# A GEGLU MLP in fp16: the first pass fed by plain fp32 loads, weight operands stored in the second pass, x scaled by 1/16

## The chip, the cores and the metric

The kernel runs on one core of a Trainium2 chip. Times are device microseconds (us) of that core, medians of several runs in its normal ("fast") state; the runs of one kernel in one round lie within about 0.2% of each other. A profile is one execution, taken by the hardware profiler; its span is 1.8 us shorter than the time of the same run. Experiments marked "one look" have a single time, so that their state can't be told. Engines: TensorE (PE in the profile, PEld its weight loads), VectorE (DVE), ScalarE (ACT), GpSimd (POOL), and the DMA issuing queue of SyncE (SP). L12 is line 12 of the kernel shown.

## The reference

```python
# x: 8 x 1024 x 1024, w_gate and w_up: 1024 x 4096, w_down: 4096 x 1024, all fp32
gate = x @ w_gate
up = x @ w_up
gate = 0.5 * gate * (1 + np.tanh(np.sqrt(2 / np.pi) * (gate + 0.044715 * gate ** 3)))
h = gate * up
return (h @ w_down).astype(np.float32)
```

## The kernel before

The kernel takes the 8192 rows of x in eight passes of 1024. A pass has a gate/up stage of 16 pairs of weight blocks and a down stage. Every matrix product is done as a 2x2 block scheme with seven products instead of eight, so the matmuls need sums and differences of blocks: of x (`t1` to `t4`, once per pass), of the weights (`sums_w`), and of w_down (`wd_sums`). All matmuls are fp16, 128 rows by 512 columns.

Weights arrive as fp32 in memory. Before the change they are cast on the way by GpSimd DMAs; the finished operands (raw blocks and sums) are written to memory once and read back in later passes. x is cast in memory and then transposed by DMA.

```python
WSRC = 3
...
def cast_x(p):                       # fp32 -> fp16, in memory, 2 MiB
    nc.gpsimd.dma_start(out=xh[r, :], in_=x2[r, :])
def transpose_x(p):                  # four transposing DMAs
    for n, kh, mh in (...):
        nc.sync.dma_start_transpose(out=xq[n], in_=xh[...])
...
def load_w(p, i):
    for w in range(2):
        c = ring.tile([P, 4096], FP16, tag="ring", name="wc")      # 6 buffers: three pairs
        if from_source(p, i):
            nc.gpsimd.dma_start(out=raw(c), in_=w_v[w][:, :, ...])  # casting
        else:
            nc.sync.dma_start(out=c, in_=wop[w][i])
def from_source(p, i): return p < 2 or (p == 2 and i < NP // 2)
def keeps(p, i):       return (p == 1 and i >= NP // 2) or (p == 2 and i < NP // 2)
...
# in pass 0, eight times, once per 21 products: w_down is loaded (casting, GpSimd), summed on
# VectorE 14 to 17 products later, and stored from SP as seven transfers
(0, wd_load), (14, wd_sums 0), (15, wd_sums 1), (16, wd_sums 2), (17, wd_sums 3), (17, wd_store)
...
# in a pair: 14 products, each of 4 matmuls into a PSUM bank; a bank is accumulated over several
# products, and between two of them ScalarE copies it out ("snap")
after = {1: [snap s1 gate], 2: [snap s1 up], 4: [snap s2 gate], 5: [snap s2 up], 7: ..., 8: ...}
...
cast_x(0); load_w(0, 0); load_w(0, 1); transpose_x(0); sums_x(); sums_w(0, 0, 0); sums_w(0, 0, 1)
```

The order in the code is the order on each engine: nothing is rescheduled, and an engine's instruction that waits holds back all behind it.

## Time and profile before

| | before |
|---|---|
| time, median of 3 | 2420.92 us |
| span of the profile | 2422.5 us |
| TensorE busy | 2335.6 us (96%), 10752 matmuls |
| VectorE, ScalarE, GpSimd busy | 42%, 34%, 24% |
| operand stores | pass 1 (half), pass 2 (half) |

A busy share near 100% hides the losses. It is read better as a floor: what a stage takes beyond 0.2158 us for each of its matmuls is its loss. The **loss at the start** is the time at which the first product with a difference of x begins, less 8 x 0.2158 us for the eight matmuls that can run before it. The **loss of pass 0** is the time from there to the first matmul of the down stage, less 888 x 0.2158 = 191.6 us. Before, these times are 54.78 and 277.96 us: losses 53.1 and 31.5. Pass 1 loses nothing, pass 2 13.6, the end 4. All these losses come from one profile each, so differences of some 3 us between two profiles are not read.

### The profile page before, as it was taken

The page shows a single profiled execution, that of the slowest core. Times are in us where ns is not written, and L with a number is a line of the kernel's source. Part 1 is how long each engine was busy: PE and PEld are TensorE (multiplying, and loading weights), DVE is VectorE, ACT ScalarE, POOL GpSimd, SP SyncE. Part 2 cuts the span into 40 slices and gives each one's busy share as a digit, 9 for nine tenths or more (in the row PEclk, how much of TensorE's full clock was granted, in tenths as well). Part 3 has the DMA queues.
Part 4 walks back from the last instruction along what each step waited for, and adds up shares of the span by engine and source line. Part 5 has one row for each costly group of instructions (what it writes and reads, how often), then busy time and mean ns, then how long its engine had stood idle before and what let it go on. Part 6 is the DMA issues. An engine that isn't in the chain of part 4 may idle for free.

```text
span 2422.5 us, 27727 instructions
## 1 busy us (share of the span) xinstructions
PE 2335.6 (96%) x10752; PEld 1055.0 (44%) x10752; DVE 1027.3 (42%) x1504; ACT 830.1 (34%) x1410; POOL 577.8 (24%) x484
## 2 busy tenths in 40 slices
PE   1979999999998999999999999999999999999999
PEld 0434444444443444444444444444444444444444
DVE  1757625666163351333513344233522335233350
ACT  0434304442143421444114440244403443044420
POOL 1444203441042310333003330133201332023310
PEclk8989999999998999999999999999999999999999
DMA  9999666998797465544756455564645645554453
GB/s 152 180 204 211 177 195 97 175 262 272 170 272 239 174 218 194 204 185 174 225 194 206 177 186 193 215 209 176 206 166 221 210 175 187 210 197 174 175 187 109
DMA packets 230405, 469.49 MB, mean 194 GB/s; under 512 B 76160, under 2 KB 164224, under 8 KB 188800
## 3 DMA queue, kind: packets, MB, share of 16 engines
q1 hardware_dynamic: 142208, 400.59, 46.2%
q0 software_dynamic: 88064, 67.12, 19.1%
q8 instruction: 84, 1.38, 0.2%
q14 instruction: 49, 0.40, 0.1%
HBM read 436.21 MB, written 98.57 MB: 221 GB/s over the span
## 4 chain that ended last, share of the span: by engine, by line
PE 90%; DMA 7%; SPq 1%; DVE 1%; issue 0%; POOL 0%; ACT 0%; POOLq 0%; DVEq 0%; ACTq 0%
PE ps_a L241 33%; PE ps_da L375 18%; PE ps_b L241 17%; PE ps_db L375 9%; PE ps_c L241 8%; PE ps_dc L375 5%; DMA h_s<-in_w_down_dram 3%; DMA wd_ops<-h_s 2%; SPq L91 1%; DMA wc<-in_w_up_dram 1%; DMA x_half<-in_x_dram 1%; DMA x_b<-x_half 0%; SPq L189 0%; DVE t L255 0%; DVE h_s L170 0%
## 5 line engine op out<-in xcount | busy, mean ns | idle before, releaser
L241 PEld LDWEIGHTS <-wc 128*128 128x128 f16 x7168 | 704.3, 98 | 940.6 <-issue 63.3
L261 POOL TENSOR_TENSOR h_a<-t 128x512 f16<-128x512 f32 x384 | 496.7, 1294 | 1510.8 <-DVE t L255 1414.5
L241 PE MATMUL ps_a<-x_t,wc 128*128 128x512 f16 x3072 | 728.3, 380 | 12.4 <-ACT t L248 12.4
L248 ACT ACTIVATE t<-ps_a 128x512 f32<-128x512 f32 x768 | 458.0, 597 | 499.1 <-PE ps_a L241 499.1
L253 DVE TENSOR_TENSOR t<-ps_b,t 128x512 f32<-128x512 f32 x256 | 176.9, 691 | 691.6 <-ACT t L248 671.3
L375 PEld LDWEIGHTS <-h_a 128*128 128x128 f16 x3072 | 300.6, 98 | 362.5
L258 ACT ACTIVATE t<-t 128x512 f32<-128x512 f32 x384 | 240.9, 627 | 326.0 <-DVE t L253 325.3
L375 PE MATMUL ps_da<-dc,h_a 128*128 128x512 f16 x1536 | 335.4, 379 | 0.0
L347 ACT ACTIVATE o<-ps_da 128x512 f32<-128x512 f32 x128 | 76.4, 597 | 698.0 <-PE ps_da L375 698.0
L241 PE MATMUL ps_b<-x_t,wc 128*128 128x512 f16 x1024 | 264.5, 381 | 21.5 <-DVE wc L142 21.5
L241 PE MATMUL ps_a<-x_b,wc 128*128 128x512 f16 x1024 | 246.8, 385 | 29.8 <-DMA x_b<-x_half 29.8
L241 PE MATMUL ps_b<-x_b,wc 128*128 128x512 f16 x1024 | 246.2, 384 | 19.7 <-DVE t L253 19.7
L241 PE MATMUL ps_c<-x_b,wc 128*128 128x512 f16 x1024 | 262.8, 379 | 0.0
L375 PE MATMUL ps_db<-dc,h_a 128*128 128x512 f16 x1024 | 223.6, 379 | 0.0
L255 DVE SCALAR_TENSOR_TENSOR t<-ps_b,t 128x512 f32<-128x512 f32 x256 | 177.0, 691 | 40.1 <-PE ps_b L241 21.8
L350 DVE SCALAR_TENSOR_TENSOR o<-ps_db,o 128x512 f32<-128x512 f32 x64 | 44.3, 692 | 328.2 <-ACT o L347 244.9
L264 DVE SCALAR_TENSOR_TENSOR h_a<-ps_a,t 128x512 f16<-128x512 f32 x128 | 88.5, 691 | 83.3 <-PE ps_a L241 80.0
L375 PE MATMUL ps_dc<-dc,h_a 128*128 128x512 f16 x512 | 111.8, 379 | 0.0
L375 PE MATMUL ps_da<-dc,h_s 128*128 128x512 f16 x512 | 111.8, 379 | 0.0
L354 DVE TENSOR_TENSOR h_a<-h_a,h_a 128x2048 f16<-128x2048 f16 x96 | 110.2, 1214 | 0.0
L269 ACT ACTIVATE t<-ps_a 128x512 f32<-128x512 f32 x128 | 76.3, 596 | 65.6 <-PE ps_a L241 65.6
L255 DVE SCALAR_TENSOR_TENSOR t<-ps_c,t 128x512 f32<-128x512 f32 x128 | 88.4, 691 | 11.9
(26 smaller groups left out, 516.7 us busy)
## 6 DMA issues: line engine op xcount, KB each, us to landing
wc<-w_ops SPq DMA_DIRECT2D x176, 1024.0 KB, 6.4
dc<-wd_ops SPq DMA_DIRECT2D x112, 1024.0 KB, 6.5
out_dram<-o SPq DMA_DIRECT2D x128, 256.0 KB, 2.4
w_ops<-wc SPq DMA_DIRECT2D x32, 1024.0 KB, 9.1
wc<-in_w_gate_dram POOLq DMA_DIRECT2D x40, 512.0 KB, 8.0
wc<-in_w_up_dram POOLq DMA_DIRECT2D x40, 512.0 KB, 13.1
x_half<-in_x_dram POOLq DMA_DIRECT2D x8, 2048.0 KB, 15.2
wd_ops<-h_s SPq DMA_DIRECT2D x56, 256.0 KB, 7.8
```

Source lines behind the costliest of these rows:

```text
L241: nc.tensor.matmul(ps, lhs(k), rhs[:, k, :], start=(first and k == 0), stop=(k == KH - 1), skip_group_check=True,)
L248: nc.scalar.activation(tl((n, w)), bank["a", w], COPY, scale=1.0 if w == 0 else HSC)
L253: nc.vector.tensor_tensor(o, bank[b, w], o, ADD)
L255: nc.vector.scalar_tensor_tensor(o, bank[b, w], HSC, o, MUL, ADD)
L258: nc.scalar.activation(t[n, 0], t[n, 0], GELU)
L261: nc.gpsimd.tensor_tensor(hq[h][:, i, :], t[n, 1], t[n, 0], MUL)
L264: nc.vector.scalar_tensor_tensor(hq["a12"][:, i, :], bank["a", 1], HSC, t["gl21"], MUL, MUL)
L269: nc.scalar.activation(tl("gl21"), bank["a", 0], GELU)
L347: nc.scalar.activation(tl((n, g)), bank["a", g], COPY, scale=OSC)
L350: nc.vector.scalar_tensor_tensor(t[n, g], bank[b, g], OSC, t[n, g], MUL, ADD)
L354: nc.vector.tensor_tensor(hq[o][:, s, :], hq[a][:, s, :], hq[b][:, s, :], op)
L375: nc.tensor.matmul(bank[b, g], lhs[:, j, g * P : (g + 1) * P], dc[:, n, :], start=(first and j == 0), stop=(j == NP - 1), skip_group_check ...
```

## The change

Intent: let the first pass start sooner and keep GpSimd's casting queue free. x of pass 0 is loaded plainly and transposed on TensorE; the weights of pass 0 are loaded plainly into two fp32 staging buffers and cast on ScalarE; all 16 pairs of operands are stored in pass 1 and none in pass 2; and x is scaled by 1/16 so that the up branch needs no scale of its own.

```diff
+    stage = ctx.enter_context(tc.tile_pool(name="stage", bufs=2))
+    def scale_x():                       # passes 1 to 7, in the down stage
+        for n in ("b11", "b12", "b21", "b22"):
+            nc.vector.tensor_scalar(xq[n], xq[n], XSC, None, MUL)
+    def x0_transpose(mh, g):             # one block of 128 rows, eight of them
+        if g % 2 == 0:
+            nc.vector.tensor_scalar(h, f, XSC, None, MUL)      # cast
+        else:
+            nc.scalar.activation(h, f, COPY, scale=XSC)        # cast
+        for k in range(2 * KH):
+            nc.tensor.transpose(ps[:, k], h[:, k * P : (k + 1) * P], identity)
+        nc.vector.tensor_copy(xq[...][:, :, c], ps[:, 0:KH])
+        nc.scalar.copy(xq[...][:, :, c], ps[:, KH : 2 * KH])
 ... load_w
+            if p == 0:
+                f = stage.tile([P, 2 * KH, 2 * P], FP32, tag="stage", name="wf")
+                nc.sync.dma_start(out=f, in_=w_v[w][:, :, ...])
+            elif from_source(p, i):
+    def cast_w(i, w, kh):                # four a pair: after products 4, 7, 10 and 13, for pair i + 2
+            nc.scalar.copy(raw(chunks[0, i, w])[:, k], staged[i, w][:, k])
     def from_source(p, i):
-        return p < 2 or (p == 2 and i < NP // 2)
+        return p < 2
     def keeps(p, i):
-        return (p == 1 and i >= NP // 2) or (p == 2 and i < NP // 2)
+        return p == 1
 ... (scales: snap, add and h21 lose HSC, the GELUs get scale=16)
-    cast_x(0)
-    load_w(0, 0)
-    load_w(0, 1)
-    transpose_x(0)
 ...
+    x0_load(0, 0); x0_load(0, 1); load_w(0, 0); x0_load(0, 2); x0_load(0, 3)
+    for g in range(G): x0_load(1, g)
+    load_w(0, 1)
+    for g in range(G): x0_transpose(0, g)
+    for n in (0, 2, 1, 3): cast_w(0, n // 2, n % 2)
```

(Some statements are joined on one line here. The transposes of the second half of x, `x0_rest`, come after the second product of the first pair.)

More of the change, by code (lines that the diff above doesn't have):

```diff
@@ L6 @@
 from concourse._compat import with_exitstack
+from concourse.masks import make_identity
 FP32 = mybir.dt.float32
@@ L14 @@
 COPY = mybir.ActivationFunctionType.Copy
-HSC = 1.0 / 16.0
+XSC = 1.0 / 16.0
+GSC = 16.0
 OSC = 16.0
@@ L50 @@
     G = MH // P
-    WSRC = 3
     w_v = [w.rearrange("(kc k) n -> k kc n", k=P) for w in (w_gate, w_up)]
@@ L79 @@
     }
+    identity = const.tile([P, P], FP16, name="identity")
     ctx.enter_context(tc.manual_schedule())
+    make_identity(nc, identity)
     def cast_x(p):
@@ L93, in transpose_x, with sum_x, x0_load @@
             )
-    def sums_x():
-        t = nc.vector.tensor_tensor
-        t(xq["t1"], xq["b12"], xq["b11"], SUB)
-        t(xq["t2"], xq["b22"], xq["t1"], SUB)
-        t(xq["t3"], xq["b22"], xq["b12"], SUB)
-        t(xq["t4"], xq["b21"], xq["t2"], SUB)
+    def scale_x():
+        for n in ("b11", "b12", "b21", "b22"):
+            nc.vector.tensor_scalar(xq[n], xq[n], XSC, None, MUL)
+    def sum_x(n):
+        o, a, b = {
+            1: ("t1", "b12", "b11"), 2: ("t2", "b22", "t1"),
+            3: ("t3", "b22", "b12"), 4: ("t4", "b21", "t2"),
+        }[n]
+        nc.vector.tensor_tensor(xq[o], xq[a], xq[b], SUB)
+    x0_f32 = {
+        mh: hq[n].rearrange("p a b -> p (a b)").bitcast(FP32).rearrange(
+            "p (t k) -> p t k", t=G
+        )
+        for mh, n in ((0, "a11"), (1, "a21"))
+    }
+    x0_f16 = hq["a12"].rearrange("p (t a) b -> p t (a b)", t=2 * G)
+    def x0_load(mh, g):
+        r0 = mh * MH + g * P
+        nc.sync.dma_start(out=x0_f32[mh][:, g], in_=x2[r0 : r0 + P, :])
+    def x0_transpose(mh, g):
+        f, h = x0_f32[mh][:, g], x0_f16[:, mh * G + g]
+        if g % 2 == 0:
+            nc.vector.tensor_scalar(h, f, XSC, None, MUL)
+        else:
+            nc.scalar.activation(h, f, COPY, scale=XSC)
+        ps = psum.tile([P, 2 * KH, P], FP16, tag="ps", name="ps_x")
+        for k in range(2 * KH):
+            nc.tensor.transpose(ps[:, k], h[:, k * P : (k + 1) * P], identity)
+        c = slice(g * P, (g + 1) * P)
+        nc.vector.tensor_copy(xq["b11" if mh == 0 else "b12"][:, :, c], ps[:, 0:KH])
+        nc.scalar.copy(xq["b21" if mh == 0 else "b22"][:, :, c], ps[:, KH : 2 * KH])
     chunks = {}
+    staged = {}
     def raw(c):
@@ L118, in load_w @@
             chunks[p, i, w] = c
-            if from_source(p, i):
+            if p == 0:
+                f = stage.tile([P, 2 * KH, 2 * P], FP32, tag="stage", name="wf")
+                staged[i, w] = f
+                nc.sync.dma_start(out=f, in_=w_v[w][:, :, i * 2 * P : (i + 1) * 2 * P])
+            elif from_source(p, i):
                 nc.gpsimd.dma_start(
@@ L124, in load_w @@
                 nc.sync.dma_start(out=c, in_=wop[w][i])
+    def cast_w(i, w, kh):
+        if i < NP:
+            k = slice(kh * KH, (kh + 1) * KH)
+            nc.scalar.copy(raw(chunks[0, i, w])[:, k], staged[i, w][:, k])
     def from_source(p, i):
-        return p < 2 or (p == 2 and i < NP // 2)
+        return p < 2
     def keeps(p, i):
-        return (p == 1 and i >= NP // 2) or (p == 2 and i < NP // 2)
+        return p == 1
     def sums_w(p, i, w):
@@ L247, in snap @@
         def snap(n, w):
-            nc.scalar.activation(tl((n, w)), bank["a", w], COPY, scale=1.0 if w == 0 else HSC)
+            nc.scalar.copy(tl((n, w)), bank["a", w])
         def add(n, b, w):
             o = t[n, w]
-            if w == 0:
-                nc.vector.tensor_tensor(o, bank[b, w], o, ADD)
-            else:
-                nc.vector.scalar_tensor_tensor(o, bank[b, w], HSC, o, MUL, ADD)
+            nc.vector.tensor_tensor(o, bank[b, w], o, ADD)
         def gelu(n):
-            nc.scalar.activation(t[n, 0], t[n, 0], GELU)
+            nc.scalar.activation(t[n, 0], t[n, 0], GELU, scale=GSC)
         def prod(n, h):
@@ L263, in h21 @@
         def h21():
-            nc.vector.scalar_tensor_tensor(
-                hq["a12"][:, i, :], bank["a", 1], HSC, t["gl21"], MUL, MUL
-            )
+            nc.vector.tensor_tensor(hq["a12"][:, i, :], bank["a", 1], t["gl21"], MUL)
         def gelu21():
-            nc.scalar.activation(tl("gl21"), bank["a", 0], GELU)
+            nc.scalar.activation(tl("gl21"), bank["a", 0], GELU, scale=GSC)
         after = {
@@ L304, in gate_up @@
                 extra[5].append(lambda i=i: sums_w(p, i + 1, 1))
+            if p == 0 and i == 0:
+                extra[2].append(x0_rest)
             if p == 0:
+                for n, k in enumerate((4, 7, 10, 13)):
+                    extra[k].append(lambda i=i, n=n: cast_w(i + 2, n // 2, n % 2))
                 for q in range(8):
@@ L411, in down @@
                         if name == "P5":
-                            sums_x()
+                            scale_x()
+                            for n in range(1, 5):
+                                sum_x(n)
                 k = 2 * v + nb + 4
@@ L421, in down, with x0_rest @@
             f()
-    cast_x(0)
+    def x0_rest():
+        for g in range(G):
+            x0_transpose(1, g)
+        sum_x(1)
+        sums_w(0, 0, 0)
+        sum_x(2)
+        sums_w(0, 0, 1)
+        sum_x(3)
+        sum_x(4)
+        for n in range(4):
+            cast_w(1, n // 2, n % 2)
+    x0_load(0, 0)
+    x0_load(0, 1)
     load_w(0, 0)
+    x0_load(0, 2)
+    x0_load(0, 3)
+    for g in range(G):
+        x0_load(1, g)
     load_w(0, 1)
-    transpose_x(0)
-    sums_x()
-    sums_w(0, 0, 0)
-    sums_w(0, 0, 1)
+    for g in range(G):
+        x0_transpose(0, g)
+    for n in (0, 2, 1, 3):
+        cast_w(0, n // 2, n % 2)
     for p in range(NPASS):
```

## The prediction

> **What bounds the kernel now.** I read the page first: 2422.5 us, TensorE busy 96%, and a low row of PE digits only at the start. Then the chain of waits in order of time, for the pace of an undisturbed matmul; then a table by stage, the list of what TensorE waited for, the timeline of the start, and the DMA queues of the stretch that is worst.
>
> The chain shows blocks of 64 matmuls in the down stage:
>
> ```profile
> 291.94 13.81 PE ps_dc L375 x64
> 305.75 13.81 PE ps_da L375 x64
> ```
>
> 13.81/64 is 0.2158 us per matmul. There are 10752 of them, so 2320.3 us is the floor of this program on TensorE, and 102 us of the span are lost. The stage table says where (columns: window, its length, PE busy with the count of matmuls, granted clock, DMA share, GB/s):
>
> ```profile
> 0.00:60.00 60.00, 8.79 (x26) 0.83 1.05 153
> 60.00:250.00 190.00, 168.34 (x742) 0.94 1.07 193
> 250.00:700.00 450.00, 450.00 (x2087) 1.00 0.83 200
> 700.00:850.00 150.00, 139.53 (x634) 0.95 0.72 220
> 850.00:2422.50 1572.50, 1568.90 (x7270) 1.00 0.53 191
> ```
>
> Length minus count times 0.2158 us gives the losses: 54 us in the first 60, 30 us from 60 to 250 (the first pass), nothing from 250 to 700, 13 us from 700 to 850 (the third pass), 4 us at the end. The reader is to see that the DMA share is over 1 in both bad early stretches and that the other passes run at the floor. So only some 97 us can be won at all, and 84 of them lie where the change works.
>
> What TensorE waited for, over the whole run:
>
> ```profile
> PE ps_a L241 <- DMA x_b<-x_half: 29.8, 1, 29.8
> PE ps_b L241 <- DVE wc L142: 21.5, 1, 21.5
> PE ps_b L241 <- DVE t L253: 19.7, 4, 10.5
> PE ps_a L241 <- ACT t L248: 12.4, 4, 10.8
> ```
>
> The first two are one cause. The timeline shows x cast in memory, then transposed by four transfers that hold the queue for 34 us; VectorE starts its differences of x only then, and the weight sums stand behind them:
>
> ```profile
> 14.76 33.98 SPq L91 DMA_TRANSPOSE x_b<-x_half  x4
> 49.08 1.23 DVE L97 TENSOR_TENSOR x_t<-x_b,x_b 128x2048 f16<-128x2048 f16 x1 [49.08 <-DMA x_b<-x_half]
> 54.78 1.89 PE L241 MATMUL ps_b<-x_t,wc 128*128 128x512 f16 x4 [21.45 <-DVE wc L142]
> ```
>
> Only eight matmuls (1.7 us of work) come before 54.78, so 53 us are gone there. In the first pass the DMA queues are full (60 to 250):
>
> ```profile
> q0 software_dynamic: 30103, 22.71, 82.9%
> q1 hardware_dynamic: 10320, 13.90, 23.3%
> ```
>
> 82.9% and 23.3% of 190 us are 157 and 44 us, together 202 us of all 16 engines. The casting transfers write 22.71/157 = 144 GB/s, the plain stores 13.90/44 = 314 GB/s. VectorE waits for the w_down load (31.5 us in this stretch), holds back the additions that stand behind it, and TensorE then lacks a bank.
>
> **What the Trainium skill says.** (1) "TensorE: Matmul & The Clock Gate", section "Wait — 56ns, not 53.3ns?": warm matmuls of 512 columns start 215.7 ns apart, cold ones 426.7 ns. The trace agrees: 215.8 ns warm, and the first eight stand about 0.43 us apart. (2) "DMA: Bandwidth & Descriptors", section "SWDGE vs HWDGE vs iDMA": a cast in a DMA must be issued by GpSimd, a plain transfer can go over SP's hardware queue, and each DMA engine takes turns between its queues. The trace bears out that the casting queue is the dear one (144 against 314 GB/s); turns between queues it does not show directly. (3) "ScalarE: Activation LUTs", section "What ACT_TABLE_LOAD costs": an ACTIVATE takes 186 ns + 0.833 ns per element, so 1.04 us for 1024. The trace has 597 to 627 ns at 512 where the formula gives 613. (4) "VectorE: DVE Perf Modes", section "The perf-mode tier table": fp16 tensor_scalar of 2048 elements 693 ns, tensor_tensor 1224 ns; the trace has 1.22 us for the second, none of the first.
>
> **The change part by part.**
>
> *Start.* Removed: the cast of x in memory and four transposing transfers for pass 0. Added: eight plain loads of x (4 MiB) and two of the first weights (2 MiB), 8 casts (VectorE and ScalarE by turns), 64 transposes on TensorE, 16 evacuations, 4 weight casts. The transfer work up to the last of x is 6.3 MB. At the 314 GB/s of the plain stores that is 20 us; at the 6.55 MB in 58.1% of 30 us = 376 GB/s that the 8 KB rows of the later weight loads reach (window 1260 to 1290), 17 us. The first w_down load is now issued at the very start beside it: 1.05 MB at 144 GB/s, 7 us. With some 2.5 us before the first byte and 2 us to land, the last x is there at about 30 us. Behind it stand one cast (1 us), eight transposes (at most 0.11 us each, a quarter of a cold matmul), an evacuation (0.6), a difference of x (1.2) and a weight sum (0.4): 5 us. So the product that now starts at 54.8 starts at about 35. The eight matmuls before it and most transposes fit in the wait. Loss at that point 35 - 1.7 = 33.3; then 1.4 for the cold clock (before, 54.4 us are lost up to 60 and 53.05 up to 54.78) and 1 for short waits on the interleaved differences and sums: **about 36 us instead of 54**.
>
> *Rest of pass 0.* 26 weight loads lie between 60 and 250. As casts they write 13.6 MB at 144 GB/s: 95 us. As plain fp32 loads they write 27.3 MB: 87 us at 314 GB/s, 73 us at 376. The 202 us of transfer work become 180 to 194. That stretch of 190 us fitted 202 us of work (queues overlap, 1.06), so the new work needs 170 to 183 us, while TensorE needs 742 x 0.2158 = 160. Transfers still bound it, by 10 to 23 us instead of 30: I take **16**. The w_down loads also no longer queue behind weight casts in the software queue, which favours the lower end. Against it: the cast of the next x (2 MiB, 15.2 us to land) still falls in the fifth pair, and ScalarE gets four casts of 1.04 us per pair. It now has some 6.1 us (six copies of 0.6, four GELUs) of each 12.1 us pair; 10.3 us is 85%, so it is not the bound by throughput. But it is in order: the first cast of a pair stands between two bank copies.
>
> *Passes 1 and 2.* Before, eight pairs of pass 1 and eight of pass 2 keep operands (1 MiB stores, w_ops<-wc x32); now all 16 of pass 1 do. The 32 stores stay 32; the 80 casting loads become 32 plain fp32 loads in pass 0, 32 casting loads in pass 1, and 16 more loads of finished operands in pass 2. The 13 us of pass 2 arise where the x cast (fifth pair) meets loads and stores; pass 1 had the x cast without stores and lost nothing. So the wait moves to pass 1. There it has eight more such pairs behind it, each some 7.3 us of casting loads (1 MiB at 144 GB/s) and 5.6 us of plain ones (2 MiB at 376) = 12.9 us against 12.1: slightly over, as in pass 1 now, where overlap hid it. I take **16 us** there and 0 in pass 2.
>
> *Scaling.* The 691 ns additions stay 691 ns (tensor_tensor and scalar_tensor_tensor of this shape both have it), the copies lose their scale for nothing, GELU takes it for nothing. x gets four scalings of 0.69 us per pass, in a down stage where VectorE has room: 0 us. Pass 2 saves 64 weight sums of 0.42 us on VectorE: off the path, 0 us.
>
> Sum: 2320.3 + 36 + 16 + 16 + 4 = 2392 us in a profile, which runs 1 to 2 us above the median: **2391 us**, 1.2% faster.
>
> **The rivals.** (a) *ScalarE blocks in order.* Each weight load waits until its one of two staging buffers has been cast, about ten products (9 us) before the cast that needs it. A 1 MiB plain load lands in 5.8 to 6.5 us (the w_ops and wd_ops rows), but w_down stores (1.8 MB, 6 us) stand before it in the same SP queue every 1.5 pairs, and the x cast takes 15 us. Then the cast waits for its data and the bank copies wait behind it, though the weights are not due for another pair. Speaks for it: loads that landed in 8 to 13 us under load. Against: the queues are less full. If most of the eight w_down rounds cost 3 to 5 us, pass 0 loses 40 and the time is about 2415. (b) *Transfers are hidden after all*: at the high rate pass 0 loses 5, the start ends at 30 and pass 1 repeats 13: 2320 + 31 + 5 + 13 + 4 = 2373, the 2% mark. (c) *The start is not transfer-bound*: ScalarE has two x casts, four evacuations and four weight casts (8.6 us) before the first product and again before the first bank copy, with the second pair's weight loads waiting on it; if these do not overlap with the loads the start loss is 45 and the time 2400. (d) *Storing in all of pass 1* makes it transfer-bound: 0.8 us over 16 pairs on top of the x cast, 26 us instead of 16: 2401.
>
> **Range and chances.** The start must shrink by 10 to 26 us, as no chain of cast and transpose in memory is left; pass 0 may lie between 5 and 40; pass 1 between 10 and 26. These add to 2374 to 2412. Over 2% faster needs all three at their best: 0.09. Slower by 2% would need 65 us of new waits in pass 0: 0.02.
>
> **What would show it.** The start step: the product of the first x difference begins near 35 us, released by VectorE, with the last x landing near 30. The pass-0 step: from there to 250 the matmul count gives a loss of 10 to 23, the DMA share stays near 1, the software queue falls under 40% of the stretch. Rival (a): bank copies on ScalarE wait behind a weight cast that waits for a DMA from w_gate or w_up. Pass step: a stall near the fifth pair of pass 1, none in pass 2. The prediction is wrong if the plain 1 KB-row loads run well below 314 GB/s, if ScalarE's in-order waits reach TensorE in every pair, or if pass 1 falls behind from pair to pair.

## The result, and the profile after

The changed kernel takes **2431.97 us** (2431.69 to 2432.17), against 2420.92: 0.45% slower. Ratios here are the mean time of one kernel's fast runs over that of the other's fast runs of the same rounds, so not quite the ratio of the medians: 1.0045, 95% interval 1.0022 to 1.0068. It is a small loss where 1.2% of gain was forecast, and it lies outside the stated range of 2374 to 2412.

The table by stage of the changed kernel (window, length, PE busy with count, clock, DMA share, GB/s). The first row's count holds 64 transposes:

```profile
0.00:60.00 60.00, 30.05 (x148) 0.89 0.73 228
60.00:250.00 190.00, 146.50 (x623) 0.90 0.95 249
250.00:700.00 450.00, 444.37 (x2052) 1.00 0.85 231
700.00:850.00 150.00, 150.00 (x697) 1.00 0.52 192
850.00:2429.90 1579.90, 1576.08 (x7303) 1.00 0.53 191
```

The first 60 us now lose 42 us instead of 54 (84 real matmuls), the next 190 lose 56 instead of 30, 250 to 700 loses 7 instead of nothing, and 700 to 850 loses nothing instead of 13. By stage, with the exact starts:

| loss, us | start | pass 0 | pass 1 | pass 2 | end | sum |
|---|---|---|---|---|---|---|
| before | 53.1 | 31.5 | 0 | 13.6 | 3.7 | 102 |
| predicted | 33.3 | 18.4 | 16 | 0 | 4 | 72 |
| after | 38.4 | 59.9 | 7.1 | 0 | 4.0 | 109 |

(In the prediction, 2.4 us of its "start" of 36 come after the first product of a difference; they are put to pass 0 here.) What TensorE waits for, after:

```profile
PE ps_a L286 <- ACT t L293: 43.5, 10, 14.3
PE ps_x L132 <- DVE h_a L127: 16.9, 3, 10.6
PE ps_x L132 <- ACT h_a L129: 8.4, 4, 2.1
PE ps_b L286 <- DVE t L297: 5.6, 1, 5.6
```

The waits for x and for VectorE have shrunk, and one for ScalarE's bank copies (L293) has grown from 12.4 to 43.5 us. What ScalarE itself waits for in the first 330 us names the next link:

```profile
ACT wc L169 <- DMA wf<-in_w_gate_dram: 46.3, 9, 14.7
...
ACT wc L169 <- DMA wf<-in_w_up_dram: 4.2, 4, 2.6
```

L169 is the cast of a staged weight. The longest case, in the timeline (start, duration, engine, what):

```profile
107.38 2.09 SPq L234 DMA_DIRECT2D wd_ops<-h_s  x3
...
109.51 1.05 ACT L169 CAST wc<-wf 128x1024 f16<-128x1024 f32 x1
...
110.58 0.38 SPq L158 DMA_DIRECT2D wf<-in_w_gate_dram  x1
...
120.00 1.03 PE L286 MATMUL ps_a<-x_t,wc 128*128 128x512 f16 x4
...
133.76 1.04 ACT L169 CAST wc<-wf 128x1024 f16<-128x1024 f32 x1 [14.65 <-DMA wf<-in_w_gate_dram]
134.71 1.06 ACT L293 COPY t<-ps_a 128x512 f32<-128x512 f32 x2
135.34 1.86 PE L286 MATMUL ps_a<-x_t,wc 128*128 128x512 f16 x4 [14.32 <-ACT t L293]
```

The buffer is free when the cast ends at 110.56, the load goes out at 110.58, and its data are there at 133.7, 23 us later. The cast waits for it, the copy of the bank waits behind the cast, and TensorE waits for the copy. The weights concerned are for the pair after next: no matmul needs them yet.

Is it that the transfers have no time left? The whole of pass 0, from the first product of a difference to the down stage, before and after (the same columns as above; both windows end a matmul late, hence 889):

```profile
54.78:278.12 223.34, 201.67 (x889) 0.94 0.99 188
```

```profile
40.09:291.74 251.65, 207.66 (x889) 0.91 0.85 232
```

Share times length is 221 us of all 16 engines before and 214 after: the work is a little less, but now it is spread over 28 us more, with 15% of the engines' time unused. That speaks against a plain lack of bandwidth and for loads that go out or land too late. The trace has both. From the third pair on, eight of the 28 weight loads went out 1.4 to 7.9 us after the end of the cast that freed their buffer, 36 us in all; the other 20 went out within 0.1 us. Of the 50.5 us that ScalarE waited for weights, 20.0 stand before casts whose load went out late, 30.5 before casts whose load went out at once and landed late. The experiments test it.

### The profile page after: what moved, and what is told of

It is laid out like the page before. It is cut to its first block, busy times and chain, and to the rows that moved or that the text cites. A ratio compares the mean times of both kernels' runs of the same rounds, so it can differ in the third digit from the quotient of the medians.

```text
span 2429.9 us, 27885 instructions
## 1 busy us (share of the span) xinstructions
PE 2347.0 (97%) x10816; PEld 1060.8 (44%) x10816; DVE 1023.4 (42%) x1480; ACT 887.5 (37%) x1486; POOL 536.9 (22%) x437
## 4 chain that ended last, share of the span: by engine, by line
PE 91%; DMA 6%; ACT 1%; DVE 1%; issue 1%; SPq 0%; POOL 0%; DVEq 0%; ACTq 0%; POOLq 0%
PE ps_a L286 34%; PE ps_da L419 18%; PE ps_b L286 17%; PE ps_db L419 9%; PE ps_c L286 9%; PE ps_dc L419 5%; DMA wf<-in_w_gate_dram 4%; DMA wc<-in_w_up_dram 1%; DMA h_a<-in_x_dram 1%; DMA wf<-in_w_up_dram 1%; ACT wc L169 0%; ACT t L293 0%; PE ps_x L132 0%; DVE t L297 0%; DVE h_s L215 0%
## 5 line engine op out<-in xcount | busy, mean ns | idle before, releaser
L286 PE MATMUL ps_a<-x_t,wc 128*128 128x512 f16 x3072 | 735.6, 382 | 44.0 <-ACT t L293 43.5
L297 DVE TENSOR_TENSOR t<-ps_b,t 128x512 f32<-128x512 f32 x512 | 353.1, 691 | 814.9 <-ACT t L293 772.0
L293 ACT COPY t<-ps_a 128x512 f32<-128x512 f32 x768 | 448.1, 585 | 428.6 <-PE ps_a L286 428.5
L286 PE MATMUL ps_c<-x_b,wc 128*128 128x512 f16 x1024 | 267.7, 385 | 0.0
L297 DVE TENSOR_TENSOR t<-ps_c,t 128x512 f32<-128x512 f32 x256 | 175.8, 687 | 14.0 <-PE ps_c L286 1.5
L306 DVE TENSOR_TENSOR h_a<-ps_a,t 128x512 f16<-128x512 f32 x128 | 88.5, 691 | 84.5 <-PE ps_a L286 82.9
L309 ACT ACTIVATE t<-ps_a 128x512 f32<-128x512 f32 x128 | 76.4, 597 | 71.3 <-PE ps_a L286 71.1
L169 ACT CAST wc<-wf 128x1024 f16<-128x1024 f32 x64 | 64.9, 1044 | 50.5 <-DMA wf<-in_w_gate_dram 46.3
```

Of the source, the lines that this page charges most:

```text
L169: nc.scalar.copy(raw(chunks[0, i, w])[:, k], staged[i, w][:, k])
L286: nc.tensor.matmul(ps, lhs(k), rhs[:, k, :], start=(first and k == 0), stop=(k == KH - 1), skip_group_check=True,)
L293: nc.scalar.copy(tl((n, w)), bank["a", w])
L297: nc.vector.tensor_tensor(o, bank[b, w], o, ADD)
L306: nc.vector.tensor_tensor(hq["a12"][:, i, :], bank["a", 1], t["gl21"], MUL)
L309: nc.scalar.activation(tl("gl21"), bank["a", 0], GELU, scale=GSC)
```

## The experiments

Theory W: pass 0 loses because ScalarE waits, in order, for plain weight loads that land late. Rival T: the transfers of pass 0 are too much, whoever issues them. Within W three causes were to be told apart: the small staging, the x cast of 2 MiB beside the loads, and the queue in which the loads stand. All results, with losses as defined above:

| kernel | time | start | pass 0 | pass 1 | pass 2 |
|---|---|---|---|---|---|
| before | 2420.92 | 53.1 | 31.5 | 0 | 13.6 |
| after | 2431.97 | 38.4 | 59.9 | 7.1 | 0 |
| e1 casting loads | 2395.87 | 30.9 | 30.5 | 9.0 | 0 |
| e2 half tiles | 2416.18 | 39.1 | 43.6 | 7.8 | 0 |
| e3 casts of x first (one look) | 2423.74 | 30.8 | 59.8 | 6.8 | 0 |
| e4 wait moved to GpSimd (one look, wrong result) | 2410.19 | 33.5 | 43.4 | 6.9 | 0 |
| e5 six half tiles (one look) | 2412.75 | 39.6 | 38.6 | 8.2 | 0 |
| e6 = e1 + e3 | 2391.98 | 24.8 | 33.9 | 7.2 | 0 |
| e7 before + stores in pass 1 | 2414.08 | 50.6 | 34.4 | 7.7 | 0 |
| e8 = e6 + late x cast | 2373.25 | 24.9 | 22.1 | 1.3 | 0 |
| e9 after + late x cast | 2416.52 | 38.9 | 53.1 | 0.9 | 0 |
| e10 = e2 + e3 + e9 | 2385.35 | 30.4 | 28.5 | 0.7 | 0 |
| e11 loads on ScalarE's queue (one look) | 2406.26 | 39.7 | 31.9 | 8.3 | 0 |
| e12 half the bytes (one look, wrong result) | 2398.70 | 36.3 | 28.6 | 7.5 | 0 |
| e13 = e11 + e3 + e9 | 2383.26 | 32.2 | 24.6 | 0.7 | 0 |

The kernel before, run beside them, took 2420.2 to 2421.9 us.

### e1: casting loads in pass 0

```diff
-            if p == 0:
-                f = stage.tile(...); nc.sync.dma_start(out=f, in_=w_v[w][...])
-            elif from_source(p, i):
+            if from_source(p, i):        # and cast_w does nothing
```

> The changed kernel with one part undone: the weights of pass 0 come again by casting GpSimd transfers, no staging, no casts on ScalarE; the new start, the stores in pass 1 alone and the scaling stay. Theory W (in pass 0 ScalarE waits in order for fp32 weight loads that land late): the loss of pass 0 goes back from 60 us to the 30 of the kernel before, so about 2400 us, faster than both. Rival T (the new start with its w_down loads and stores merely crowds the transfers that follow it): pass 0 still loses over 45 us, about 2420.

Measured: 2395.87 us, ratio to before 0.9899 (0.9884 to 0.9914). Pass 0 is back at 30.5. So the new start, the scaling and the stores in pass 1 are a gain of 24 us together (against the kernel before in the same round), and the plain weight loads alone cost 36 us (35 between the profiles: 29.4 in pass 0 and 7.5 at the start, less 1.9 in pass 1). T in the form "the new start crowds what follows" falls.

### e2, e5: finer and deeper staging

```diff
-                f = stage.tile([P, 2 * KH, 2 * P], FP32, ...)        # two of 1 MiB
+                for kh in range(2):
+                    f = stage.tile([P, KH, 2 * P], FP32, ...)        # e2: four, e5: six of 512 KB
+                    nc.sync.dma_start(out=f, in_=w_v[w][:, kh * KH : (kh + 1) * KH, ...])
```

(e5 takes its memory from the pool of bank copies, 14 to 11; passes 3 to 7 lose nothing by it.)

> The same staging memory cut into four half tiles, each loaded by a transfer of 512 KB as soon as its own half has been cast: the load of a half may be issued a whole pair (14 products) before its cast instead of 10 to 11. Same bytes. Theory W, window: ScalarE's wait for weight loads falls from 50 us to under 25 and the time to 2405 to 2418. Rival T (the transfer engines have no time left): within 5 us of the changed kernel.

> Half tiles with six buffers instead of four (8 KB a partition more, taken from the pool of bank copies, 14 to 11). The transfer work of pass 0 is the same 214 us of all engines. Theory W: with loads issued 1.5 pairs ahead the engines stay full, pass 0 takes about 214 to 225 us and loses 22 to 33 instead of 60 (43.6 with four half tiles): span 2395 to 2405. Rival T: no further gain over four half tiles, span 2412 to 2418. If the smaller copy pool hurts, passes 3 to 7 show it.

Measured: pass 0 loses 43.6 and 38.6. In e2 ScalarE still waits 40 us for weights (27.6 gate, 12.7 up), more than the 25 forecast, though the time is in the forecast window. e5 stops short of the 22 to 33 forecast: 50% more buffers bring only 5 us. The window of staging is a part of the cause, 16 to 21 us of it, and not the whole; in e5 ScalarE's longest wait, the one beside the x cast, is 14.5 us, as in the changed kernel (14.7).

### e4: the wait moved off ScalarE

The casts read a constant tile, so that they never wait; GpSimd copies one element of each staged tile instead, and paces the loads. To make room for the constant tile, the pool of bank copies goes from 14 to 13.

```diff
-            nc.scalar.copy(raw(chunks[0, i, w])[:, k], staged[i, w][:, k])
+            nc.scalar.copy(raw(chunks[0, i, w])[:, k], fixed)
+            if kh == 1:
+                nc.gpsimd.tensor_copy(seen[:, 0:1], staged[i, w][:, 0, 0:1])
```

> Wrong result on purpose: ScalarE casts a constant tile, so it never waits for a weight load; the loads stay, and GpSimd copies one element of each staged tile in ScalarE's place, so the loads are paced as before and the wait lies on GpSimd. If ScalarE's wait in front of the bank copies is what holds TensorE, TensorE's wait for bank copies (43.5 us) goes to under 10 us and the span to 2380 to 2400. If the transfers hold everything (through w_down and its sums on VectorE), the span stays over 2415.

Measured: neither. The span is 2408.4 and pass 0 loses 43.4. TensorE still waits 32.2 us for bank copies, but ScalarE no longer waits for weights; VectorE waits for w_down, first 330 us:

```profile
DVE h_s L220 <- DMA h_s<-in_w_down_dram: 34.4, 7, 14.2
```

So taking the weight wait off ScalarE is worth 16.5 us, and then the chain of w_down (load, sums, stores, next load) is the next bound by the waits that the trace shows; in the kernel before VectorE waits 31.5 us for w_down between 60 and 250. GpSimd, which now waits for the weights, also issues the w_down loads, so this run makes that chain somewhat later than it need be; it is not a clean measure of the floor.

### e11: the queue of the loads

Same buffers, same bytes, same casts; each load is issued from ScalarE, on ScalarE's own hardware queue, right behind the cast that frees its buffer. It no longer stands behind the w_down stores in SP's queue (the expectation calls that theory HOL, head of line): the trace lists these loads under a queue of their own, q10, beside SP's q1.

```diff
             nc.scalar.copy(raw(chunks[0, i, w])[:, k], staged[i, w][:, k])
+            if kh == 1 and i + 1 < NP:
+                load_f(i + 1, w, nc.scalar)      # was nc.sync, in load_w
```

> The plain weight loads of pass 0 issued on ScalarE's own hardware queue, right behind the cast that frees their buffer, so that they stand behind no w_down store in SP's queue. Theory HOL (the stores in front, and SP waiting for the sums to store, make the loads late): ScalarE's wait for weight loads falls from 50 to under 30 and pass 0 loses under 48. Rival: bandwidth and window alone; pass 0 loses 54 to 66 as before.

Measured: pass 0 loses 31.9 instead of 59.9, one look, 2406.26 us. ScalarE's wait for weight loads falls from 50.5 to 22.0 us:

```profile
ACT wc L176 <- DMA wf<-in_w_up_dram: 13.5, 5, 9.7
ACT wc L176 <- DMA wf<-in_w_gate_dram: 8.5, 4, 2.8
```

and TensorE's for bank copies from 43.5 to

```profile
PE ps_a L295 <- ACT t L302: 21.5, 9, 9.0
```

The pass, by its stage line, is also denser than in the changed kernel (share 0.92 instead of 0.85):

```profile
41.38:264.95 223.57, 200.60 (x888) 0.97 0.92 258
```

This is the largest effect of any single edit that leaves the bytes as they are, and nearly the whole of the 28.4 us by which pass 0 had become worse. The bytes stay, so the cause lies in when the loads go out and land. The queue is not the only way to mend that: the window (e2), the queue and the late x cast (e9) are worth 16.3, 28.0 and 6.8 us of pass 0 one by one, more together than the 28.4, so they overlap; and e10 below brings pass 0 to 28.5 on SP's queue. The changed kernel's SP queue shows both ways in which it acts:

```profile
55.16 6.56 SPq L234 DMA_DIRECT2D wd_ops<-h_s  x7
61.82 0.40 SPq L158 DMA_DIRECT2D wf<-in_w_gate_dram  x1
...
78.58 8.91 SPq L234 DMA_DIRECT2D wd_ops<-h_s  x7
87.59 0.39 SPq L158 DMA_DIRECT2D wf<-in_w_gate_dram  x1
```

The load at 61.82 goes out as soon as its buffer is free, but seven stores (1.8 MB) went out just before it on the same queue: it takes 14.9 us to land. The buffer of the load at 87.59 is free at 79.71, when its cast ends; but SP then stands in the seven stores, which wait for VectorE's sums, and issues the load 7.9 us late. The two were not tested apart, but the traces say which one e11 removes: every load now goes out within 0.03 us of the end of the cast before it, where 36 us of delay stood, while the mean time to landing of the loads from the third pair on hardly moves (10.3 us in the changed kernel, 9.7 in e11; the longest 24.5 and 21.6).

### e12: half the bytes

```diff
-                nc.sync.dma_start(out=f, in_=w_v[w][:, :, ...])
+                nc.sync.dma_start(out=f[:, 0:KH], in_=w_v[w][:, 0:KH, ...])   # both casts read this half
```

> Wrong result on purpose: each plain weight load of pass 0 brings only the first half of its rows and both casts read that half; every wait, queue and instruction stays, half of the 33 MB of weight reads goes. If the bytes of the loads make the loss, pass 0 falls from 60 to under 25. If the order of waits and the x cast make it, pass 0 still loses 35 or more.

Measured: 28.6, between the two. Half the bytes also land sooner (6.3 us in the mean instead of 10.3), so this run alone does not part W from T; with e11, which has all the bytes and loses 31.9, it does: the bytes fit, if they are not held up.

### e9, e8: the cast of the next x

The cast of the next pass's x in memory (2 MiB on GpSimd's queue) moves from the fifth pair to the fifteenth in passes 0 and 1, its transposes and sums accordingly later in the down stage.

```diff
-            if i == 4 and p + 1 < NPASS:
+            if i == (14 if p < 2 else 4) and p + 1 < NPASS:
                 extra[2].append(lambda: cast_x(p + 1))
...
-                        if name == "P1":          # transposes;  sums: "P5" -> "P3"
+                        if name == ("P6" if p < 2 else "P1"):
```

> The changed kernel with only the late cast of x (as in e8): plain weight loads, staging and ScalarE casts stay. In the changed kernel one weight load beside the x cast took 23 us to land and TensorE stood 14.3 us. Theory: the 2 MiB cast holds the engines against the plain loads; pass 0 loses 40 to 46 instead of 60 and pass 1 under 3, about 2405 to 2412. Rival (the loads are late anyway, the cast only happened to be there): pass 0 loses over 52, over 2415.

> As e6, and the cast of the next x in memory in passes 0 and 1 moved from the fifth pair to the fifteenth, its transposes from the first to the third product of the down stage and the sums of x from the fourth to the sixth. Theory: the x cast is what makes the 11 us stall of pass 0 (one transfer of 2 MiB among weight and w_down loads) and the 6 to 9 us stall of pass 1; both shrink, 2373 to 2383. Rival: the transfers of pass 0 are too much with or without it, so pass 0 gains under 4 us and the whole under 10; or the down stage, with the transposes among its loads, stalls instead.

Measured in e9, on the changed kernel: pass 0 loses 53.1, only 6.8 less than with the early cast. The longest stall goes from 14.3 to 5.7 us, but the others remain: the forecast of 40 to 46 was wrong, the rival (over 52) came true, and the loads are indeed late anyway. In pass 1 the theory holds: 7.1 becomes 0.9. In e8, on the casting kernel, pass 0 goes from 33.9 to 22.1 and pass 1 from 7.2 to 1.3. e8 is the fastest kernel: **2373.25 us**, ratio to before 0.9806 (0.9791 to 0.9821). The interval leaves open whether it is 2% faster. What still holds it is, by its waits, the w_down chain; TensorE and VectorE (first 330 us):

```profile
PE ps_b L284 <- DVE t L295: 9.1, 3, 4.0
```

```profile
DVE h_s L213 <- DMA h_s<-in_w_down_dram: 20.0, 4, 7.5
```

### e3, e6: the start

```diff
-    for g in range(G): x0_transpose(0, g)
+    for g in range(G): x0_cast(0, g)             # casts first
+    for g in range(G): x0_turn(0, g)             # then transposes and evacuations
     for n in (0, 2, 1, 3): cast_w(0, n // 2, n % 2)
+    for g in range(G): x0_cast(1, g)             # and x0_rest only turns
```

> The changed kernel with the eight casts of x put ahead of the transposes and evacuations (same instructions, other order). In the changed kernel a cast stands behind the evacuation of the block before on the same engine, and the blocks go one by one: two bursts of 7.0 us (19.2 to 26.2) and 9.2 us (29.3 to 38.5). Theory: the start is a serial chain of VectorE, TensorE and ScalarE by then, not transfers; the first product of a difference of x moves from 40.1 to 32 to 36. Rival: the last x lands late enough to hold it; it stays within 2 us of 40.

> Casting GpSimd loads in pass 0 (as e1) and the casts of x ahead of the transposes (as e3). If the start is the serial chain, the product of the first difference moves from 32.6 to 26 to 29 and the time from 2396 to 2390 to 2393; if transfers hold it, it stays at 2394 to 2397.

The changed kernel's start, from its timeline:

```profile
2.76 11.56 SPq L122 DMA_DIRECT2D h_a<-in_x_dram  x6
...
19.20 0.69 DVE L127 TENSOR_SCALAR h_a<-h_a 128x1024 f16<-128x1024 f32 x1 [9.34 <-DMA h_a<-in_x_dram]
...
26.19 3.29 PE L286 MATMUL ps_a<-x_b,wc 128*128 128x512 f16 x8 [2.08 <-ACT wc L169]
...
36.93 1.04 PE L132 MATMUL ps_x<-identity,h_a 128*128 128x128 f16 x8 [2.09 <-ACT h_a L129]
...
40.09 1.89 PE L286 MATMUL ps_b<-x_t,wc 128*128 128x512 f16 x4 [2.12 <-DVE wc L187]
```

and with the casts first (e3):

```profile
28.32 2.09 PE L135 MATMUL ps_x<-identity,h_a 128*128 128x128 f16 x32
...
32.52 1.04 PE L289 MATMUL ps_b<-x_t,wc 128*128 128x512 f16 x4 [2.11 <-DVE wc L190]
```

In the changed kernel a block of x is cast, transposed and evacuated, and ScalarE's cast of the next block stands behind its evacuation of this one: the second four blocks run from 29.3 to 38.5. With the casts ahead, their 32 transposes follow each other in 2.09 us and the product of the first difference comes at 32.5 instead of 40.1, within the forecast. In e3 the last block whose cast waits for its load is cast at 24.6, so data were not the limit. With casting loads the product comes at 32.6 (e1) and 26.5 (e6), because 2 MiB of weights no longer stand between the blocks of x: in the changed kernel the load of the third block, behind them, takes 16.4 us to land.

### e7: stores in pass 1 only, on the kernel before

```diff
-        return p < 2 or (p == 2 and i < NP // 2)
+        return p < 2
-        return (p == 1 and i >= NP // 2) or (p == 2 and i < NP // 2)
+        return p == 1
```

> The kernel before with one part of the change alone: operands are stored in pass 1 only. My theory from the two traces: the 13.5 us stall of pass 2 goes and one of about 6 to 8 us comes near the fifth pair of pass 1: 2413 to 2416 us. Rival (my prediction): the stall only moves, 2420 to 2424.

Measured: 2414.08 us, ratio 0.9979 (0.9964 to 0.9993). The stall of pass 2 (13.6) becomes one of 7.7 in pass 1. Why it is smaller there was not tested. It is the only part of the change that was tried alone on the kernel before, and it gains 0.2%.

### e10, e13: the plain way at its best

> The plain-load way with all that helped: half tiles in staging (e2), casts of x hoisted (e3), late x cast (e9). It tells whether the plain way was only badly fed. If its transfers are no dearer than the casting ones (210 us of all engines against 220), it comes to a loss in pass 0 of 20 to 27 as e8 has (22) and to 2375 to 2385. If the ScalarE in-order waits stay, it loses 30 or more there and comes to 2387 to 2395, so casting loads stay better.

> e11 (plain weight loads on ScalarE's hardware queue) with the casts of x hoisted (e3) and the late x cast (e8). If the queue order was the main cause and the transfers of the plain way are no dearer than the casting ones, pass 0 loses 17 to 25, as e8's 22, and the whole is 2369 to 2379, even with e8's 2373. If the plain way has a price of its own (ScalarE at 85% and in order, more bytes), it stays over 2382, as e10's 2385, and casting loads are the better way.

Both are built from edits shown above. Measured: e10 2385.35 (0.9850, interval 0.9835 to 0.9864) and pass 0 at 28.5, just over its first forecast; e13 2383.26 (0.9841, 0.9824 to 0.9857) and pass 0 at 24.6, as forecast, but with a time over 2382, on the side of "a price of its own", because its start loses 32.2 where e8 loses 24.9. So in the steady part plain loads are hardly dearer than casting ones (24.6 against 22.1), nor are they cheaper; 7.3 of the 10 us between e13 and e8 are the start, where fp32 weights stand among the blocks of x and ScalarE must cast them.

## Why the prediction was wrong

**The pass-0 step failed.** The prediction said of the stretch from 60 to 250: "so the new work needs 170 to 183 us, while TensorE needs 742 x 0.2158 = 160. Transfers still bound it, by 10 to 23 us instead of 30: I take **16**." It lost 56 in that stretch and 59.9 in pass 0. The total of transfer work was about right: 214 us in all of pass 0 against 221 before, where the prediction saved 8 to 22 us in part of it. What failed was the assumption under it, that the transfers would stay as densely packed as before ("That stretch of 190 us fitted 202 us of work (queues overlap, 1.06)"). Before, GpSimd issued a weight load as soon as the pair began, with a ring of three pairs, a queue without stores, and VectorE as the consumer 16 products later. After, a load goes out only when its buffer has been cast, about ten products before its own cast, behind the w_down stores of SP's queue, and its consumer stands ahead of the bank copies on ScalarE. e11 shows it: the same transfers on another queue lose 31.9. So the cost of the bytes was sized about right, and the overlap was wrong: the step has no term for the time between the freeing of a buffer and the landing of its next load, 10.3 us in the mean plus up to 7.9 of late issue, against a window that the prediction itself put at 9.

**Rival (a) named this wait**, with its cause, "w_down stores (1.8 MB, 6 us) stand before it in the same SP queue every 1.5 pairs, and the x cast takes 15 us". Its sign, bank copies behind a weight cast that waits for a DMA, came true. It was given a loss of 40 and 2415 us, which already lay outside the stated range of 2374 to 2412: its wait, 50.5 us on ScalarE and 43.5 on TensorE, held TensorE in ten places, one of them for 14.3 us, where most of eight by 3 to 5 us were foreseen. What it missed is that SP's queue also blocks at issue, while the stores wait for sums.

**The start step was half right.** 35 us was forecast for the first product of a difference, 40.1 measured. The data came sooner, the last x at 25.5 instead of 30; the chain behind them was mis-sized, "5 us" for one block where four blocks went through VectorE, TensorE and ScalarE one after the other in 9.2. e3 puts it right by order alone. Rival (c), that ScalarE's order holds the start, was the better description.

**The step on passes 1 and 2 had the right direction and too large a size.** The stall of pass 2 went, as said, and one came in pass 1: 7.1 us instead of 16. e7 shows the same change alone at 7.7, and e9 that the x cast makes nearly all of it. Rival (d) falls: pass 1 did not fall behind from pair to pair. The sum behind it, 12.9 us a pair, also put the operand stores at the 376 GB/s of loads, though the only plain stores it had measured ran at 314; with these it would have been 14.0, and further off.

**The scaling step was right**: no stall in any later pass, and the 691 ns of the additions are the same in both profiles. The 28 scalings of x took 685 to 692 ns, which bears out at fp16 the 693 that the prediction cites (the page's column is for bf16).

The sum: start 5 us worse than forecast, pass 0 41.5 worse, pass 1 9 better. That is 37.5, and the span is 2429.9 instead of the 2392 forecast for it. The stated range does not follow from its own parts either: with a start of 28 to 44, pass 0 of 5 to 40 and pass 1 of 10 to 26, the floor and the end, they add to some 2366 to 2433, not 2374 to 2412. The measured 2431.97 would just have lain inside that, but by luck: pass 0 alone left its part by 20 us, and pass 1 fell below its own.

What stays open: how much of TensorE's loss is due to late issue and how much to late landing (only ScalarE's waits are divided above), why the same stall is smaller in pass 1 than in pass 2, and how much a w_down chain freed of its stores would still give e8.

## What to carry to other kernels

Before moving loads to another queue, list what stands before each of them in that queue and what those wait for; taking loads of equal bytes off a queue shared with stores that wait for results gained 28 us of pass 0 here. When a copy or cast that waits for a DMA is put on an engine that frees banks, the wait becomes TensorE's, even though no matmul needs the data yet; keep such waits behind the work that frees banks, or on another engine. An estimate from total transfer time holds only if the transfers can still be issued early enough to fill it: count the products between the freeing of a buffer and its next use, and set the time to landing under load beside it.

## What the Trainium skill lacked or had wrong

- "DMA: Bandwidth & Descriptors", section "Issuing engines are not separate DMA queues", says that issuing from several engines only saves the sequencer's issue time. In this case moving 30 loads from SP's queue to ScalarE's, with all bytes the same, took 28.0 us out of pass 0 (59.9 to 31.9, one look). That section leaves out what stands before a load on its issuing engine: stores that wait for results hold the loads behind them back, here by 36 us in all, up to 7.9 us each.
- "TensorE: Matmul & The Clock Gate", section "Part 4: PE-mode transpose", gives some 275 ns for a 128x128 transpose inside a kernel. Here one takes 219 to 315 ns in the trace, but 32 in a row span 2.09 us in e3 (65 ns apiece) and 3.18 us in e6, and eight in a row 0.61 to 1.04 us: the page's figure is the duration of one, and the spacing of a stream of transposes is missing.
- No page has what a casting transfer of 2 MiB in memory does to the loads beside it: with it, two weight loads took 23.2 and 24.5 us to land, and moving it gave 11.8 us in pass 0 and 5.9 in pass 1 between e6 and e8.
